# A row-wise roll in HBM: the last 256 rows in four large DMAs, where they were 32 DMAs of half rows

## The chip, the cores and the metric

One core of a Trainium2 chip (trn2). The metric is the device time of one execution in microseconds (us). A profile's own span is 2.1 to 2.2 us shorter than the device time listed for the same execution.

## The reference

```python
def setup_inputs():
    return {"x": np.random.randn(8192, 8192).astype(np.float32), "shift": 100}

def reference(x, shift):
    return np.roll(x, shift, axis=1)
```

Every row of 32,768 bytes moves 100 columns to the right; the last 100 columns come round to the front. Nothing is computed: 268 MB are read and 268 MB written.

## The kernel before

With a shift of 100, columns 256 to 8191 of the output (31,744 bytes a row) are copied from HBM to HBM by the DMA queues of SyncE and ScalarE. The first 256 columns go through on-chip memory by GpSimd's queue. The last of its DMAs is issued at 374 us and its last packet starts at 485 us; the change does not touch them. This is the wide copy:

```python
    engines = [nc.sync, nc.scalar]
    # ...
    xm = x.rearrange("(c e j) w -> c j e w", e=16, j=4)
    om = out.rearrange("(c e j) w -> c j e w", e=16, j=4)
    if a < n_cols:                       # a = 256, s = 100
        blocks = n_rows // 64            # 128
        mid = (a + n_cols) // 256 * 128  # 4224
        for c in range(blocks):
            parts = ((a, mid), (mid, n_cols)) if c >= blocks - 4 and a < mid else ((a, n_cols),)
            for j in range(4):
                for lo, hi in parts:
                    engines[j % 2].dma_start(out=om[c, j, :, lo:hi], in_=xm[c, j, :, lo - s:hi - s])
    # ... the first 256 columns, by nc.gpsimd
```

A DMA takes 16 rows (`e`), one for each of the core's 16 DMA engines. Two DMAs of each 64-row block go to each queue. In the last four blocks each is cut in two: 16 DMAs of half rows a queue. A DMA is issued only when the one four places earlier in its queue has landed (its bytes have arrived and its completion is counted) on all 16 engines. I call the four in flight the window.

## Time and profile before

| | before |
|---|---|
| median of the first three runs | 829.27 us (829.12 to 830.45) |
| span of the profiled execution | 817.9 us |
| DMA engines busy | 99.3% |
| moved, HBM read plus write | 656 GB/s |

Two rows of the page matter besides those that the prediction shows. The first gives the GB/s of the span's 40 slices, the second the DMA packets:

```profile
GB/s 307 333 348 342 347 355 347 355 356 344 350 338 363 359 351 354 361 346 360 334 333 341 326 335 331 331 332 337 328 338 331 330 336 331 335 334 326 331 308 299
DMA packets 21572, 276.89 MB, mean 339 GB/s; under 512 B 9024, under 2 KB 9024, under 8 KB 13120
```

From 409 us on, when little is left of the narrow columns, the rate is 326 to 341 GB/s. It falls in the last two slices (20 us each), where the half rows are. The 9024 packets under 512 bytes are the engines' completion writes.

The end is best read backwards from the last landing, here 816.9 us. These are the stages from 60 us before it; the last two columns are the DMA share and GB/s. The view books a packet's whole time where it starts, so a share can pass 1 and the last stretch reads a little low:

```profile
756.90:776.90 20.00, 0.00 (x0) 0.00 (x0) 1.00 1.00 332
776.90:804.90 28.00, 0.00 (x0) 0.00 (x0) 1.00 0.92 318
804.90:810.90 6.00, 0.00 (x0) 0.00 (x0) 1.00 0.98 336
810.90:816.90 6.00, 0.00 (x0) 0.00 (x0) 1.00 0.75 254
```

Before pays in the 28 us stretch (0.92, 318 GB/s), in which the halved window leaves engines idle. Its last 6 us are still at 254 GB/s.

### The profile page before, as it was taken

Reading aid. Unit: us, or ns where it says so; the run is one execution under the profiler, and the core shown is the slowest. Engines: PE = TensorE matmul, PEld = TensorE weight load, DVE = VectorE, ACT = ScalarE, POOL = GpSimd, SP = SyncE. Lnnn points to the kernel's source line nnn. Section 1 sums busy time; section 2 is a strip of 40 time slices with the busy share of each in tenths; the row PEclk is TensorE's granted clock in tenths of the full one; section 3 lists DMA queues with packets and bytes.
Section 4 is the critical chain, followed back from the end, with each engine's and each line's share of the span. In section 5 each row is a group of like instructions: output and inputs, shape, how many; then the busy total and the mean of one; then the engine's idle time right before and its main releaser. Section 6 shows DMA issues by size and latency. Waiting matters only on the chain. (4 is left out here: it accounts for less than half of the span.)

```text
span 817.9 us, 633 instructions
## 1 busy us (share of the span) xinstructions
DVE 7.7 (1%) x8; POOL 28.9 (4%) x40
## 2 busy tenths in 40 slices
DVE  0000000000000000000000000000000000000000
POOL 3000000010010000000000000000000000000000
DMA  9999999999999999999999999999999999999998
GB/s 307 333 348 342 347 355 347 355 356 344 350 338 363 359 351 354 361 346 360 334 333 341 326 335 331 331 332 337 328 338 331 330 336 331 335 334 326 331 308 299
DMA packets 21572, 276.89 MB, mean 339 GB/s; under 512 B 9024, under 2 KB 9024, under 8 KB 13120
## 3 DMA queue, kind: packets, MB, share of 16 engines
q10 hardware_dynamic: 8448, 130.04, 46.5%
q1 hardware_dynamic: 8448, 130.04, 45.9%
q0 software_dynamic: 4672, 16.78, 6.9%
q14 instruction: 4, 0.03, 0.0%
HBM read 268.44 MB, written 268.44 MB: 656 GB/s over the span
## 5 line engine op out<-in xcount | busy, mean ns | idle before, releaser
L82 POOL DMA_DIRECT2D out_dram<-h x16 | 13.2, 827 | 196.6 <-DMA out_dram<-h 112.1
L73 POOL DMA_DIRECT2D t<-in_x_dram x12 | 9.5, 795 | 60.4 <-DMA h<-in_x_dram 30.1
L75 DVE COPY h<-t 128x1200 f32<-128x1200 f32 x4 | 3.1, 785 | 233.6 <-DMA t<-in_x_dram 233.6
L78 DVE COPY h<-t 128x1872 f32<-128x1872 f32 x4 | 4.9, 1224 | 0.0
L74 POOL DMA_DIRECT2D h<-in_x_dram x4 | 3.0, 749 | 45.6 <-DMA t<-in_x_dram 45.6
L77 POOL DMA_DIRECT2D h<-in_x_dram x4 | 3.0, 751 | 42.8 <-DMA t<-in_x_dram 42.8
L99 POOL MEMSET const-float32-0.0<- 128x1 f32 x1 | 0.1, 100 | 0.2 <-issue 0.2
L99 POOL MEMSET const-bfloat16-1.0<- 128x1 bf16 x1 | 0.1, 103 | 0.0
L99 POOL MEMSET const-float32-1.0<- 128x1 f32 x1 | 0.1, 100 | 0.0
L99 POOL MEMSET const-uint8-127<- 128x1 uint8 x1 | 0.1, 100 | 0.0
## 6 DMA issues: line engine op xcount, KB each, us to landing
out_dram<-in_x_dram ACTq DMA_DIRECT2D x248, 496.0 KB, 12.7
out_dram<-in_x_dram SPq DMA_DIRECT2D x248, 496.0 KB, 12.7
out_dram<-h POOLq DMA_DIRECT2D x16, 512.0 KB, 112.6
t<-in_x_dram POOLq DMA_DIRECT2D x12, 512.0 KB, 95.4
out_dram<-in_x_dram SPq DMA_DIRECT2D x16, 248.0 KB, 5.7
out_dram<-in_x_dram ACTq DMA_DIRECT2D x16, 248.0 KB, 5.9
h<-in_x_dram POOLq DMA_DIRECT2D x4, 312.0 KB, 92.0
h<-in_x_dram POOLq DMA_DIRECT2D x4, 200.0 KB, 97.9
```

The costliest lines, as they stand in the source:

```text
L73: nc.gpsimd.dma_start(out=t[:, q - 1], in_=lead)
L74: nc.gpsimd.dma_start(out=h[:, Q - 1, :, :s], in_=xt[k, Q - 1, :, :, n_cols - s:])
L75: nc.vector.tensor_copy(h[:, :Q - 1, :, :s], t[:, :, :, :s])
L77: nc.gpsimd.dma_start(out=h[:, 0, :, s:], in_=xt[k, 0, :, :, :g])
L78: nc.vector.tensor_copy(h[:, 1:, :, s:], t[:, :, :, s:])
L82: nc.gpsimd.dma_start(out=ot[k, q, :, :, :a], in_=h[:, q])
L99: nc = _bacc.Bacc("TRN2", target_bir_lowering=False, num_devices=1)
```

## The change

The intent: the last 256 rows go out in four DMAs of whole rows, four rows an engine each. They are all in the queues some 30 us before the end, with no further waits between the engines and 28 fewer issues.

```diff
-        mid = (a + n_cols) // 256 * 128
-        for c in range(blocks):
-            parts = ((a, mid), (mid, n_cols)) if c >= blocks - 4 and a < mid else ((a, n_cols),)
+        for c in range(blocks - 4):
             for j in range(4):
-                for lo, hi in parts:
-                    engines[j % 2].dma_start(out=om[c, j, :, lo:hi], in_=xm[c, j, :, lo - s:hi - s])
+                engines[j % 2].dma_start(out=om[c, j, :, a:], in_=xm[c, j, :, a - s:n_cols - s])
+        xt = x.rearrange("(t c e j) w -> t j e c w", c=4, e=16, j=4)
+        ot = out.rearrange("(t c e j) w -> t j e c w", c=4, e=16, j=4)
+        t = blocks // 4 - 1
+        for j in range(4):
+            engines[j % 2].dma_start(out=ot[t, j, :, :, a:], in_=xt[t, j, :, :, a - s:n_cols - s])
```

## The prediction

> **What bounds the kernel now.** I read the page's busy shares first, then its queue table, the queue's waits, the issues, and last the stages of the end. The busy shares rule out compute; the row of DMA shares and the queue table show who works:
>
> ```profile
> DVE 7.7 (1%) x8; POOL 28.9 (4%) x40
> DMA  9999999999999999999999999999999999999998
> q10 hardware_dynamic: 8448, 130.04, 46.5%
> q1 hardware_dynamic: 8448, 130.04, 45.9%
> q0 software_dynamic: 4672, 16.78, 6.9%
> HBM read 268.44 MB, written 268.44 MB: 656 GB/s over the span
> ```
>
> The sixteen DMA engines are busy 46.5 + 45.9 + 6.9 = 99.3% of 817.9 us; only the last slice is under nine tenths. q1 and q10 (SyncE's and ScalarE's) carry the wide copy; q0 (GpSimd's narrow columns) is 6.9% and does nothing at the end. So the time is bytes over bandwidth, and an edit of DMA shapes can win only what the engines idle: 0.7% of the span, 5.7 us, at most, unless the bandwidth itself changes.
>
> ```profile
> out_dram<-in_x_dram ACTq DMA_DIRECT2D x248, 496.0 KB, 12.7
> out_dram<-in_x_dram SPq DMA_DIRECT2D x248, 496.0 KB, 12.7
> out_dram<-in_x_dram SPq DMA_DIRECT2D x16, 248.0 KB, 5.7
> out_dram<-in_x_dram ACTq DMA_DIRECT2D x16, 248.0 KB, 5.9
> SPq L43 <- DMA out_dram<-in_x_dram: 671.1, 259, 3.9
> ```
>
> The issues show the changed part: two times 16 DMAs of 248 KB. The last line, from the queue's waits, says that SyncE waited for an earlier DMA before 259 of its 264 issues. The program's order says for which: each DMA waits on one of eight completion semaphores, four a queue, so DMA n waits for DMA n-4 of its queue. Four are in flight in each queue: 8 rows an engine while they are rows, 8 half rows at the end. The stages of the end and the times to landing (380 to 780 us, then 797 to 816 us) show what that does:
>
> ```profile
> 560.00:791.00 231.00, 0.00 (x0) 0.00 (x0) 1.00 0.99 331
> 791.00:797.00 6.00, 0.00 (x0) 0.00 (x0) 1.00 0.81 291
> 797.00:814.00 17.00, 0.00 (x0) 0.00 (x0) 1.00 0.96 338
> 814.00:817.90 3.90, 0.00 (x0) 0.00 (x0) 1.00 0.35 118
> ...
> DMA to landing us min/median/max: 10.5/12.4/13.3
> ...
> DMA to landing us min/median/max: 4.9/5.8/6.6
> ```
>
> The last two columns are DMA share and GB/s. Where half rows begin there is a hole (0.81), then almost full speed (0.96, 338 GB/s), then a ramp down. The hole is the halved window: half the bytes in flight are eaten in half the time, and engines that are ahead run dry until the slowest lets the next DMA go.
>
> **How far apart the engines are** decides this case. The trace records the sixteen completion counts of each DMA. In SyncE's DMAs 180 to 239 (counted from 0) the first engine was on average 7.1 us ahead of the last; sorted, twelve engines lead the last one by 3.7 to 7.1 us (mean 5.3), and four by 0 to 0.9 us. The last whole-row DMA (247) landed first at 787.2 and last at 794.3 us on SyncE's queue, 794.5 on ScalarE's. With the half rows that spread fell to 1.0 to 2.5 us, and the last landings are at 816.5 and 816.9.
>
> **What the Trainium skill says.** (1) "DMA: Bandwidth & Descriptors", section "Why a DMA increments its semaphore by 16 and not by 1": the number of engines is the largest up to 16 that divides the slowest dimension of both patterns. That is 16 before and after, so the new DMA gives each engine four rows, and no engine's bytes change. The trace agrees for before: 264 DMAs x 16 x (one row, one completion write) = 8448 packets. (2) The same page, section "Rules for kernel authors", advises at least 1 MiB a DMA for bandwidth. The trace does not support this here: 248 KB DMAs ran at 338 GB/s from 797 to 814 us, 496 KB ones at 331, because several overlap. (3) "HBM Reference", section "Specifications (TRN2)", gives some 716 GB/s for the pair of cores. The copy's 656 GB/s (reads and writes) is 92% of that, so I take memory contention as the bound of the steady part. In favour: the trace's shortest packet of a row is 1.174 us, while the mean from 380 to 780 us is (50.2 + 48.9)% x 16 x 400 us / 4162 rows = 1.52 us.
>
> **The change part by part.**
> - *Removed:* 32 DMAs of 16 half rows. Their issues take 0.51 us each, 16 x 0.51 = 8 us a queue, all beside running transfers: no gain. Their waits: the last 12 half-row issues of a queue were gated by a half-row landing. This made the hole: 6 us x (0.99 - 0.81) = 1.1 us, and 17 us x (0.99 - 0.96) = 0.5 us. Together 1.6 us of idle engine time, a mean over sixteen engines.
> - *Added:* four DMAs of 1984 KB, two a queue. The first waits for DMA 244 of its queue (landed 785.2 us), the second for 245 (788.4 us). From 788.4 us everything is in the queues and nothing gates any engine.
> - *Moved:* the engines' wait for one another goes from the hole to the end. Every engine must move 16 more rows after its row of DMA 247 (8 a queue), as before; nothing takes rows from a slow engine. The slowest has 16 left at 794.4 us. The twelve leading ones have 5.3 / 1.52 = 3.5 fewer: 12.5.
> - *Sum:* all sixteen run at 1.52 us a row until the leading ones finish: 12.5 x 1.52 = 19.0 us. The slow four then have the memory to themselves, and I give them the shortest packet: 3.5 x 1.174 = 4.1 us. The end is 794.4 + 19.0 + 4.1 = 817.5 us, against 816.9 before. In truth the leaders finish one by one over 3.4 us and relieve the rest sooner; a small calculation with all sixteen leads, 333 to 338 GB/s in all and 27 GB/s an engine gives 817.0 to 817.3. So **+0.1 to +0.6 us**. The closing part (1.0 us after the last landing) stays. The unprofiled median is 829.27 us; I add 0.3 us: **829.6 us**.
>
> Why so little: before, the leading engines idle in the middle and the slow ones catch up while memory is free; after, the same happens at the end. The slowest engine's own list of rows sets the end both times.
>
> **The rivals.**
> - *The hole is pure loss.* If the slowest engine also idled through it, all 1.6 us come back: 829.3 - 1.6 = 827.7 us. For it: the share of 0.81. Against it: the spread before the hole, by which the slow four had work left when the others ran dry.
> - *The slow four are slow by themselves,* not by contention. Then they keep 1.52 us a row: 16 x 1.52 = 24.3, end at 818.7, +1.8 us: 831.1 us. For it: the spread stays for hundreds of us. Against it: in the half rows the last engine did 16 rows in 22.5 us (794.4 to 816.9), 1.41 us a row, waits included.
> - *Large DMAs run faster or slower.* An engine now takes four rows, 64 rows apart, in a run from one queue. The packets stay 31,744 bytes, so I expect nothing. If they were slower by 5%, the last 8.1 MB (24 us at 334 GB/s) would cost 1.2 us.
> - *Issues too late.* If a DMA of 64 rows took long to be expanded, leading engines would starve near 787 us. They have a lead of several us to lose, so under 1 us at the end.
>
> **Range and chances.** The rivals span 827.7 to 831.1 us, the three runs of before 829.12 to 830.45. I widen both sides by about half a us: 827.2 to 831.7. A change of 2% is 16.6 us, three times all the idle time of the DMA engines; only a surprise of bandwidth outside the last 3% of the bytes could make it. Faster 0.01, same 0.98, slower 0.01.
>
> **What would show the steps right or wrong.** In the profile after: four issues of 1984 KB; the DMA share from 791 to 797 us back near 0.99 (right: no hole); a longer ramp down, with the share falling from about 811 us and only some four engines busy after 814 us (right: the waiting moved to the end); the last landing near 817 us. The mean row packet should shorten towards 1.174 us in those last us; if it stays near 1.5 us, the slow engines are slow by themselves. If the last landing is at or below 815.5 us, the hole was pure loss. If the share falls before 788 us, issue starved the engines. A steady part (before 780 us) that differs from 331 to 334 GB/s would be a difference of runs and not of the change, since the first 496 wide DMAs are identical; it could make the prediction wrong either way.

## The result, and the profile after

After: 831.21 us median of 6 runs (830.27 to 833.63). Before, in the same rounds and the three first runs: 829.35 us (827.41 to 830.45). The ratio is 1.0019, 95% interval 1.0000 to 1.0039: the same by the 2% rule, and probably slower by a little. The ratios and intervals can differ from the ratio of the means of all runs listed (1.0028 here).

The profiled execution of after has a span of 830.2 us, 12 us over the profile of before. Most of that is not the change: the last landing of the rows before the last 256 was at 805.4 us, against 794.5 us, though both kernels issue the same wide DMAs up to there. The page, then the stages at fixed times, then the same stages backwards from the last landing at 829.0 us:

```profile
DMA  9999999999999999999999999999999999999997
q10 hardware_dynamic: 8096, 130.04, 46.5%
q1 hardware_dynamic: 8096, 130.04, 45.5%
out_dram<-in_x_dram SPq DMA_DIRECT2D x2, 1984.0 KB, 26.5
out_dram<-in_x_dram ACTq DMA_DIRECT2D x2, 1984.0 KB, 26.5
```

```profile
560.00:791.00 231.00, 0.00 (x0) 0.00 (x0) 1.00 1.00 328
...
797.00:814.00 17.00, 0.00 (x0) 0.00 (x0) 1.00 1.00 329
814.00:817.00 3.00, 0.00 (x0) 0.00 (x0) 1.00 1.00 317
817.00:820.00 3.00, 0.00 (x0) 0.00 (x0) 1.00 1.03 349
820.00:823.00 3.00, 0.00 (x0) 0.00 (x0) 1.00 0.76 265
823.00:826.00 3.00, 0.00 (x0) 0.00 (x0) 1.00 0.49 212
826.00:829.00 3.00, 0.00 (x0) 0.00 (x0) 1.00 0.13 53
```

```profile
789.00:817.00 28.00, 0.00 (x0) 0.00 (x0) 1.00 0.99 324
817.00:823.00 6.00, 0.00 (x0) 0.00 (x0) 1.00 0.89 307
823.00:829.00 6.00, 0.00 (x0) 0.00 (x0) 1.00 0.31 132
```

The hole is gone: the DMA share is 1.00 from 797 to 820 us. In its place stands a long ramp down, 0.76, 0.49, 0.13, and the last 6 us move 132 GB/s where before moved 254. On SyncE's queue the last DMA landed first at 820.5 us and last at 828.9 us, a spread of 8.3 us between the engines (7.4 us on ScalarE's; in before 1.5 and 1.0 us).

The loss can be counted in bytes. Take the steady 331 GB/s of before as full and read the three stretches of the last 40 us. Before lost 28 x (1 - 318/331) + 6 x (1 - 336/331) + 6 x (1 - 254/331) = 1.1 - 0.1 + 1.4 = 2.4 us. After lost 28 x (1 - 324/331) + 6 x (1 - 307/331) + 6 x (1 - 132/331) = 0.6 + 0.4 + 3.6 = 4.6 us. That is 2.2 us more, from one profile each.

### The profile page after: what moved, and what is told of

The parts are those of the page before. It is cut to its first block, busy times and chain, and to the rows that moved or that the text cites. A ratio compares the mean times of both kernels' runs of the same rounds, so it can differ in the third digit from the quotient of the medians. Undisturbed runs are those within 1.5% of the kernel's fastest.

```text
span 830.2 us, 605 instructions
## 1 busy us (share of the span) xinstructions
DVE 7.7 (1%) x8; POOL 28.8 (3%) x40
```

## The experiments

One theory and three rivals were to be told apart.

- **Theory:** the sixteen engines enter the last 256 rows 6 to 8 us apart. Each has a fixed list of rows. Gating by half rows brings them together before the end; without it they stop one after another.
- **Rival 1:** nothing at the end matters, the difference is run-to-run variation of the steady part.
- **Rival 2:** the large ungated DMAs themselves cost time or part the engines.
- **Rival 3:** the half *packets* make the end even, not the gating.

For all kernels the trace gives two measures. The *spread* is the time from the first to the last of the sixteen completion counts of the last DMA, given for the two queues. The *idle time* is that of a mean engine in the 40 us before the last landing: the packets' times clipped to that stretch, summed, divided by 16 and taken from 40 us. It lies about 1 us under what the stages' shares give, because these book a packet at its start. Differences are of the mean times to those of before in the same rounds, with the standard error. Kernels timed in the same rounds share the runs of before, so their differences are not independent.

| kernel | time less before, us | ratio (95%) | spread at the end, us | idle, last 40 us |
|---|---|---|---|---|
| before (two profiles) | | | 1.0 to 1.5 | 3.0, 3.3 |
| after (first result) | +2.3 +/- 0.7 | 1.0019 (1.0000 to 1.0039) | 7.4, 8.3 | 4.1 |
| after_again | +1.1 +/- 0.7 | 1.0012 (0.9994 to 1.0029) | 7.1, 8.4 | 4.3 |
| whole | +2.1 +/- 0.7 | 1.0024 (1.0006 to 1.0041) | 4.7, 6.0 | 3.8 |
| free_half | +1.5 +/- 0.7 | 1.0021 (1.0004 to 1.0038) | 7.8, 9.0 | 3.9 |
| free1024 | +3.7 +/- 0.6 | 1.0043 (1.0026 to 1.0059) | 15.6, 16.7 | 5.1 |
| half1024 | 0.0 +/- 0.8 | 1.0001 (0.9981 to 1.0021) | 1.3, 1.9 | 1.1, and a hole earlier |
| all_half | +2.8 +/- 1.0 | 1.0046 (1.0025 to 1.0066) | 1.0, 1.8 | 1.5 |
| all_big | +15.6 +/- 1.7 | 1.0190 (1.0159 to 1.0220) | 30.1, 32.9 | 12.2 |
| together | +0.9 +/- 0.6 | 1.0014 (0.9994 to 1.0034) | 2.5, 2.5 | 2.0, and a hole earlier |
| low12 | +2.5 +/- 0.6 | 1.0030 (1.0013 to 1.0047) | lists differ | 4.4 |
| low8 | +1.5 +/- 0.8 | 1.0020 (1.0001 to 1.0039) | lists differ | 5.4 |
| low4 | +2.9 +/- 0.9 | 1.0036 (1.0017 to 1.0056) | lists differ | 3.2 |

The twelve runs made after the first result are correct to the reference (after_again is the kernel of the first result).

### after_again and before_again: is there a difference at all?

No edit in either.

> The changed kernel as it is, timed in the same rounds as the others. Tail = from the last landing of the rows before the last 256 to the last landing of all: 22.5 us in the profile of before, 23.6 us in that of after. If the tail is what differs, the median lies 0.5 to 2.0 us above before and the tail is again 23.2 to 24.2 us with a spread of the sixteen engines of 7 to 9 us in the last DMA. If the +1.9 us of the first result was the steady part's run-to-run variation, the median lies within 0.5 us of before.

> The kernel before, profiled once more, because its first profile (span 817.9 us) is of an execution some 8 us shorter than its timed runs. The steady part should be 5 to 12 us longer than in that profile; the end the same in form: a hole where the half rows begin, spread at the end 1 to 2.5 us, tail (from the last landing before the last 256 rows to the last landing) 22.0 to 23.2 us.

after_again: 830.95 us median of 6 (829.52 to 833.42), before 830.25 us of 11 (828.04 to 832.30). With the first result there are 12 runs of after (mean 831.4 us) and 17 of before (829.8 us): +1.6 us, standard error 0.5. So rival 1 is unlikely (the interval of after_again alone still includes 1), but the size is known only to about a microsecond. The end came out as in the first profiles. The time from the last landing of the rows before the last 256 to the last of all is 23.6 and 23.5 us for after, 22.5 and 23.0 us for before. before_again's span is 827.3 us (one look, so of unknown state), 9.4 us longer than the first profile of the same kernel. Its stages up to 60 us before the end are up to 5 GB/s slower, which confirms that the 12 us between the first two profiles were mostly not the change. Its end, and that of after_again:

```profile
786.40:814.40 28.00, 0.00 (x0) 0.00 (x0) 1.00 0.91 309
814.40:820.40 6.00, 0.00 (x0) 0.00 (x0) 1.00 0.95 333
820.40:826.40 6.00, 0.00 (x0) 0.00 (x0) 1.00 0.77 246
```

```profile
787.30:815.30 28.00, 0.00 (x0) 0.00 (x0) 1.00 1.00 330
815.30:821.30 6.00, 0.00 (x0) 0.00 (x0) 1.00 0.97 323
821.30:827.30 6.00, 0.00 (x0) 0.00 (x0) 1.00 0.20 85
```

By the same count of bytes before_again lost 1.9 + 0.0 + 1.5 = 3.4 us and after_again 0.1 + 0.1 + 4.5 = 4.7 us: 1.3 us more. The two pairs of profiles give 2.2 and 1.3 us, the timed runs 1.6 us. The shape is clear, before pays in the 28 us stretch and after in the last 6 us; the size stays within these bounds.

### whole: neither large nor halved

```diff
-            parts = ((a, mid), (mid, n_cols)) if c >= blocks - 4 and a < mid else ((a, n_cols),)
+            parts = ((a, n_cols),)
```

> The last 256 rows as the rest: DMAs of 16 whole rows, four in flight a queue, nothing large and nothing halved. Theory (the slowest engine's own list of rows sets the end, and what counts is how far apart the engines are when they stop): spread at the end 5 to 8 us, tail 23.0 to 24.0 us, time like after, +0.5 to +2 us over before. Rival (the cost of after lies in the large ungated DMAs themselves): tail 22.5 us or less, time like before.

832.31 us median of 6 (829.87 to 834.08): +2.1 us, like after. There is no large DMA in it, so rival 2's cost of large DMAs is not needed. The spread (4.7 and 6.0 us) is at the lower edge of what was expected (5 to 8), a little less than in after. The 22.5 us from the last landing before the last 256 rows is a miss, by 0.5 us: it equals before's first profile and is what the rival had named. This length depends on where the slowest engine happens to stand at its start and is the weaker measure. The last 6 us show the cost all the same:

```profile
825.00:831.00 6.00, 0.00 (x0) 0.00 (x0) 1.00 0.26 106
```

### free_half: half packets without the gating

```diff
-            engines[j % 2].dma_start(out=ot[t, j, :, :, a:], in_=xt[t, j, :, :, a - s:n_cols - s])
+            for lo, hi in ((a, mid), (mid, n_cols)):
+                engines[j % 2].dma_start(out=ot[t, j, :, :, lo:hi], in_=xt[t, j, :, :, lo - s:hi - s])
```

> The last 256 rows in eight DMAs of half rows, four half rows an engine each, so the packets are halved as in before but all are in the queues by about the time the fourth-last whole-row DMA lands. Theory (only the gating brings the engines together): spread at the end 6 to 9 us, tail 23.0 to 24.2 us, like after. Rival (the half packets make the end even or fast): spread under 3 us, tail 22.5 us, like before.

831.38 us median of 6 (829.47 to 833.30): +1.5 us, spread 7.8 and 9.0 us, 23.1 us from the last landing before the last 256 rows. The packets are as small as in before, and the end is that of after:

```profile
820.40:826.40 6.00, 0.00 (x0) 0.00 (x0) 1.00 0.33 132
```

Rival 3 falls; it is the gating by the small window.

### free1024: four times as long without gating

```diff
-        for c in range(blocks - 4):
+        for c in range(blocks - 16):
...
-        xt = x.rearrange("(t c e j) w -> t j e c w", c=4, e=16, j=4)
-        ot = out.rearrange("(t c e j) w -> t j e c w", c=4, e=16, j=4)
-        t = blocks // 4 - 1
+        xt = x.rearrange("(t c e j) w -> t j e c w", c=16, e=16, j=4)
+        ot = out.rearrange("(t c e j) w -> t j e c w", c=16, e=16, j=4)
+        t = blocks // 16 - 1
```

> The last 1024 rows in four DMAs, sixteen rows an engine each: the engines run ungated four times as long. Theory in its strong form (the window of four DMAs holds the leading engines back in favour of the slow ones): the spread at the end grows to 12 to 25 us and the time is 3 to 8 us over before. Weak form (the engines' speeds are alike and the spread is only carried along): spread 6 to 10 us, time within 1 us of after.

833.99 us median of 6 (831.77 to 835.01): +3.7 us, spread 15.6 and 16.7 us. The strong form holds: left alone, the engines drift apart. The spread is not a fixed offset but is held to some 7 us by the window. What makes some engines lag is not shown by any run.

### all_big: the changed form throughout

```diff
-        for c in range(blocks - 4):
+        for c in range(0):
...
-        t = blocks // 4 - 1
-        for j in range(4):
-            engines[j % 2].dma_start(out=ot[t, j, :, :, a:], in_=xt[t, j, :, :, a - s:n_cols - s])
+        for t in range(blocks // 4):
+            for j in range(4):
+                engines[j % 2].dma_start(out=ot[t, j, :, :, a:], in_=xt[t, j, :, :, a - s:n_cols - s])
```

> The changed form throughout: DMAs of 64 rows, four rows an engine, four in flight a queue, so a window of 32 rows an engine and queue... in all four times that of before. If the window bounds how far the engines part, the spread in the steady part grows from 6 to 7 us to 15 to 40 us, and the time by 2 to 15 us through the end. If the engines' speeds are alike, the spread stays under 10 us and the time within 2 us of after.

845.14 us median of 4 (842.46 to 849.87): +15.6 us, 1.9% slower, just over the 2 to 15 us expected. With a window of four times the rows, the last DMA before the final two of SyncE's queue has a spread of 39 us. The end, backwards from the last landing at 843.1 us:

```profile
803.10:831.10 28.00, 0.00 (x0) 0.00 (x0) 1.00 0.87 311
831.10:837.10 6.00, 0.00 (x0) 0.00 (x0) 1.00 0.33 143
837.10:843.10 6.00, 0.00 (x0) 0.00 (x0) 1.00 0.09 37
```

For the last 12 us most engines have nothing left. The idle time of the last 40 us is 12.2 us, 9 us over before. That is most, not all, of the +15.6 us; where the rest goes is not shown.

### half1024 and all_half: gating earlier, and always

```diff
-            ... if c >= blocks - 4 and a < mid else ((a, n_cols),)
+            ... if c >= blocks - 16 and a < mid else ((a, n_cols),)      # half1024
+            parts = ((a, mid), (mid, n_cols))                           # all_half
```

> Half rows from the last 1024 rows on, where before has them in the last 256. Theory (the halved window brings the engines together once, at the cost of one hole, and then holds them together at full speed): the hole moves to about 725 us, spread at the end again 1 to 2.5 us, time within 0.8 us of before. Rival (each half-row DMA costs idle time: share 0.96 for as long as they last): four times the idle time, 2 to 3 us over before.

> Half rows throughout. If the even engines of the half-row stage (338 GB/s against 331 in the same profile) are a better steady state, the time falls by 0.5 to 2 %. If the half window idles the engines, above all beside the narrow columns' DMAs in the first 370 us, it rises by 0.5 to 3 %. No hole at the end in either; spread at the end under 3 us.

half1024: 829.39 us median of 6 (828.51 to 833.18), no difference from before; the rival's 2 to 3 us did not come. The hole moved to where the half rows now begin, and the end is as even as in before:

```profile
725.00:735.00 10.00, 0.00 (x0) 0.00 (x0) 1.00 0.84 287
735.00:745.00 10.00, 0.00 (x0) 0.00 (x0) 1.00 0.98 332
745.00:780.00 35.00, 0.00 (x0) 0.00 (x0) 1.00 0.99 325
```

So one hole buys an even end whenever it is paid, and holding the engines together afterwards costs too little to see in 100 us. Over the whole kernel a cost is seen: all_half took 833.54 us median of 4 (830.24 to 834.06), +2.8 us or 0.46% by the ratio, just under the slower of the two cases expected; the faster one fell. Where the time goes is not shown: the profiled execution is the fastest of the four (830.24 us), 0.8 us longer in span than before_again's. One candidate stands in the trace: each DMA puts a completion write of 9 ns on each of its engines, and with 1024 wide DMAs in place of 528 these take 9.3 us of each engine in place of 4.8 us. Twice as many packets of half the size are another; no run tells them apart.

### together: bring the engines together, then let them go

```diff
         for c in range(blocks - 4):
+            parts = ((a, mid), (mid, n_cols)) if c >= blocks - 8 else ((a, n_cols),)
             for j in range(4):
-                engines[j % 2].dma_start(out=om[c, j, :, a:], in_=xm[c, j, :, a - s:n_cols - s])
+                for lo, hi in parts:
+                    engines[j % 2].dma_start(out=om[c, j, :, lo:hi], in_=xm[c, j, :, lo - s:hi - s])
```

> Both forms in a row: half rows for the 256 rows before the last 256, to bring the engines together, then the changed form (four DMAs of four rows an engine) for the last 256. Theory (the spread is carried into the last 256 rows, the large DMAs do not make it): the hole of about 1.6 us moves to 766 to 780 us, the spread at the end is 2 to 4 us in place of 7 to 8, and the idle time of the last 12 us is 1.5 to 2.5 us in place of 4.0 to 4.3. Rival (large ungated DMAs part the engines by themselves): spread 6 us or more at the end and idle time as in after, on top of the hole. Time within 1 us of after in the first case, 1 us or more over after in the second.

The hole came at 775 to 785 us, a little later than expected. This kernel has the same four large DMAs as after, but the engines enter them 1.5 and 2.0 us apart. They leave them 2.5 us apart, and the idle time of the last 12 us is 1.6 us, against 4.0 and 4.3 us in after's two profiles:

```profile
775.00:785.00 10.00, 0.00 (x0) 0.00 (x0) 1.00 0.85 306
...
814.20:820.20 6.00, 0.00 (x0) 0.00 (x0) 1.00 0.93 317
820.20:826.20 6.00, 0.00 (x0) 0.00 (x0) 1.00 0.62 222
```

The spread is carried in; large DMAs do not make it within 24 us. As a cause of the spread, rival 2 falls. The time, 830.84 us median of 6 (829.61 to 832.54) against 830.41 us, cannot be told from either kernel.

### low12, low8, low4: unequal lists

Here the last 256 rows are dealt unevenly, by two DMAs whose slowest dimension is 12, 8 or 4. The core of low12 (low8 and low4 have other counts, so that the sum stays 256):

```diff
+        # 192 rows as 12 an engine, in four DMAs; 16 rows as two DMAs of half rows; then:
+        for q in engines:
+            tail(q, slice(r, r + 24), a, n_cols, e=12)   # rows "(c e) w -> e c w"
+            r += 24
```

> The changed form, but the last 256 rows are not dealt evenly: twelve engines get 17 rows and the other four 13, by two DMAs whose slowest dimension is 12. Theory (the slowest engine's own list sets the end): if the four lagging engines are the four with 13 rows, the end comes 2 to 3 us earlier than in after, at or under before, and the idle time of the last 40 us falls from 4.2 us to 1.5 to 2.5 us; if they are among the twelve, the end comes 1.2 to 1.5 us later and the idle time grows to 5 to 6 us. If the lists do not matter, both stay as in after. It is not known beforehand which engines lag.

> Eight engines get 18 rows, the other eight 14. Theory: if all lagging engines are among the 18s, the end comes 2.4 to 3.0 us later than in after; if all are among the 14s, 1 to 2 us earlier; if some are in each group, later as in the first case. If the lists do not matter, as after.

> Four engines get 19 rows, the other twelve 15. Theory: if a lagging engine is among the four, the end comes 3.5 to 4.5 us later than in after; if none is, the lagging ones have one row less and the end comes about 1.2 us earlier, with the four at 19 rows finishing near it. If the lists do not matter, as after.

In low12's trace only 12 or 13 engines move data 9 us before the end, where after has 16; in low8's trace 12, and 8 at 6.5 us before the end. So the lists do shape the end. But the times (+2.5, +1.5, +2.9 us, each within 0.6 to 0.9 us) do not follow the idle times (4.4, 5.4, 3.2 us), and none lies where one of the stated cases puts it clearly. From the last landing before the last 256 rows to the end they took 23.4, 25.8 and 23.9 us, against 23.6 and 23.5 us in after: low8's profile comes near the case that lagging engines had the long lists, low12's the case that the lists do not matter. Which engines lag, and that the slowest one's list alone sets the end, is not shown by these three. They are inconclusive.

## Why the prediction was right

- **The bound** (bytes over memory bandwidth, the engines all but always busy). The rate held: in after the stages from 400 us to the end's start stand at 328 to 330 GB/s, as in before's second profile (327 to 332). That the engines share a limit is shown by the third and fourth points; that it is the memory, no run tests.
- **The hole goes, and its waiting moves to the end.** Right: the share is 1.00 where the hole had been, then 0.76, 0.49, 0.13. together and free_half show that it is the gating that had brought the engines together. The picture of four slow engines held only roughly: 3.5 us before the last landing eight packets were in flight in after and two in after_again.
- **The slow engines are not slow by themselves.** Right: in after's last 6 us (823 to 829 us) the two queues' shares are 16.0% and 14.9% for 25 row packets, so (0.160 + 0.149) x 16 x 6 / 25 = 1.19 us a row. They speed up as soon as the others are done; the rival at 831.1 us had them stay at 1.52 us. That the median of the first result was 831.21 us is no support for it.
- **The sum** was mis-sized, inside the stated range. I gave the change +0.1 to +0.6 us. The runs give +1.6 us (standard error 0.5) and the bytes 2.2 and 1.3 us. The prediction's own measure, from the last landing before the last 256 rows to the end, gives less, +0.5 to +1.1 us (23.6 and 23.5 us against 22.5 and 23.0 us). The term at fault is "the same happens at the end", for an idle engine costs less in the hole than at the end. The small calculation kept 333 to 338 GB/s in all down to thirteen engines. The traces have less: in the last 40 us of all fourteen, the packets in flight moved 331 GB/s together while there were sixteen of them, 304 with 13, 290 with 12, 212 with eight and 105 with four. So an engine short of sixteen costs some 10 GB/s at first and its full 27 GB/s (a row in 1.174 us) below about eleven. The calculation redone with these rates ends at 817.5 to 817.7 us, which is +0.6 to +0.8 us. What is left up to +1.6 us cannot be told from noise.
- **The readings.** The prediction's sums come out again from the trace. One reading is a little off: with the half rows the spread fell to 1.0 to 2.7 us, not 2.5, and only from the fourth such DMA on.
- **The rivals.** "The hole is pure loss" fell: nothing came back. "Issues too late" fell: the share is full from 797 us on. "Large DMAs run faster or slower" fell: in after they moved 329 GB/s from 797 to 814 us, where the 231 us up to 791 us had 328, and in together they left the end even.
- **The range** held, with the change's cost somewhat larger than said. The other part of the range was for runs: the profiled spans of before alone differ by 9.4 us, of which the prediction had no view. That the centre, 829.6 us, came within 1.6 us of the median rests on its being counted from the timed runs and not from the short profile.

No kernel tried beats before beyond the noise; half1024 equals it.

## What to carry to other kernels

In this kernel sixteen engines each have a fixed list; what the end costs is how far apart they arrive there, and the depth of the queue in bytes sets how far apart they may drift. It is worth some 0.2% here between before and after, and 1.9% with all_big. In a kernel of this kind, let the queue be deep enough to keep the engines fed, and make it shallower shortly before the end, while other engines can still use part of the bandwidth that an idle one leaves. For differences of a few per mille read the end backwards from its last landing: two profiles of the same kernel may differ by more than the change.

## What the Trainium skill lacked or had wrong

- "DMA: Bandwidth & Descriptors", section "Rules for kernel authors", asks for 128 partitions and at least 1 MiB a DMA for bandwidth. For this copy from HBM to HBM, with several DMAs in flight, the size was no gain: 1984 KB DMAs throughout took 1.9% longer than 496 KB ones.
- The same page, section "Latency and other measured facts", notes that DMA engines 7 and 15 are usually slower than the others. No page that I looked up says how far engines drift apart on equal lists, or that the bytes in flight bound it. The runs show a spread of mostly 4 to 9 us with four 496 KB DMAs in flight in each of two queues, 1 to 3 us with four of 248 KB, 15.6 to 16.7 us after 1024 ungated rows, and up to 42 us with four of 1984 KB. These traces do not name the engines that lag.
- The same page, section "Anatomy of one DMA — SWDGE (gpsimd) path", calls the completion write's cost on trn2 about one cycle, without saying of which clock. Traces book 9 ns of engine time for each, in the queues of SyncE and ScalarE and in GpSimd's too (9.3 ns on average in before). With 1024 wide DMAs these took 4.5 us more of each engine than with 528; whether that made all_half slower is not shown.
